# Banks returned earlier, one pool of places, memory keys after the projection and memory tokens also given transposed: a two-layer decoder trunk on one core

## The chip, the cores and the metric

The kernel runs on one core of a Trainium2 chip, in float32 and in the fp32r form of it that TensorE takes at one column per cycle. The metric is the time of one execution on the device in microseconds. PE is TensorE, DVE is VectorE, ACT is ScalarE, POOL is GpSimd and SP is the queue that issues nearly all DMAs.

## What is computed

Two layers act on x, 256 tokens of 1024 features. Each layer does three things in turn, each with a pre-RMS-norm and added to x.

- The mixer. In layer 0 it is one input projection for two groups of eight heads (A: an indexer scores all keys and each query keeps the best 64; B: causal attention within one block of 256) and one output projection over both. In layer 1 it is 16 heads in four groups with three branches (compressed blocks, selected blocks, a window), mixed by gates.
- Cross-attention with four heads of 128 to 256 memory tokens. The memory has its own RMS norm with a gain per layer; keys are normed per head.
- A SwiGLU feed-forward of width 2816.

```python
for i in range(DEPTH):
    h = rms_norm(x, norm_mix[i])
    x = x + (dsa_moba_mixer if i % 2 == 0 else nsa_mixer)(h, ...)
    x = x + memory_cross_attention(rms_norm(x, norm_mem[i]), rms_norm(mem, norm_mem_src[i]), ...)
    x = x + swiglu(rms_norm(x, norm_ffn[i]), ffn_w_in[i], ffn_w_out[i])

def memory_cross_attention(h, m, w_q, w_kv, w_o, q_norm, k_norm):
    q = rms_norm((h @ w_q).reshape(B, S, 4, 128), q_norm)
    k, v = _split(m @ w_kv, (512, 512))
    k = rms_norm(k.reshape(B, M, 4, 128), k_norm)
    p = softmax(einsum('bshd,bmhd->bhsm', q, k) * 128 ** -0.5)
    return einsum('bhsm,bmhd->bshd', p, v).reshape(B, S, 512) @ w_o
```

## The kernel before

**Tiles and matmuls.** The 256 tokens are two halves, t = 0 and 1, of 128 partitions. Every product with weights is done in three fp32r matmuls: the activation is split into a high and a low part, so is the weight, and high x high, high x low and low x high are added in one bank (mm3). A weight block is a list of units, each of two blocks of 128 input rows by up to 512 columns. A unit comes by DMA into one of three buffers `raw`; `pusher` writes its high part on ACT or DVE and its low part on DVE into one of six pairs `whl`. `gemm` takes one of two PSUM banks `mm`, walks over the units of its block and hands the bank to an evacuation thread `ev`; `both` does it for the two halves. The order of the weight blocks is the list that plan_block fills.

**Who sets the order.** The kernel is a set of generators (threads) run when it is built. Each yields an operation with an estimate of its cost on one or two engines, or a condition that must hold. `Steps.run` takes, at each step, the operation that can start first by the estimates in `Est` (within a small margin the one of the lowest rank; the main program has rank 4, evacuations and attention 2), and issues it. That fixes each engine's instruction order. On the chip the engines then run their lists in order and wait for each other's semaphores. A buffer is given back (`free`) when its last reader is issued, and until then no thread that wants it goes on. `haste` gives the pusher rank 0 only for the unit that the main program stands at, and 5 for those ahead of it.

**Buffers.** Four families of 2 KB per partition have fixed counts: 23 `slab` for queries, keys, memory, attention outputs and feed-forward activations, four `t2`, three `sn`, four `pt`, two `gv`. `t4` has two of 4 KB. PSUM has two banks each for `mm`, `sp` (scores), `tp` (transposes) and `po` (attention outputs).

**Layer 0's mixer** runs the blocks s (the indexer and A's key and value), aq, bk, bq, bv through `gemm`. Their evacuations copy the bank, square it, take the root of the mean square per head (`inv_rms`; the power on POOL), rotate, split and transpose. In `inv_rms` the bank is read by the copy and the square, but `free` is called by the caller after `inv_rms` has issued the power. `index` and `top` work out A's mask; `attention` does A for t = 0 and 1, then B. When the four pairs of heads of one branch and half are done, `finish` takes two slabs and splits the result into them (oT). After bq the thread `mem_prep` starts: it loads the memory (two DMAs of 512 KB into t4), squares it, transposes it in eight groups of four per two layers, multiplies by the gain on the way out of PSUM (`evac_gain`, through a `gv`) and splits into eight slabs (mT), which are held until the memory's values are done.

**The main program** (line 1502 on) does, per layer: the mixer, `mem_k` (the memory's key block: 24 matmuls per half of 128 memory tokens), `project` (the output projection: per half of the mix width and per t, waiting for that oT, 12 matmuls for each of two column blocks), `mem_attn` (query block mq, value block mv, output block mo) and `ffn`. The norm for the queries starts when the projection has been added to x.

Of the kernel before, what the change touches and what calls it, by code (L numbers as in the profile page):

```python
# [15 lines left out]
P = 128  # L16
D = 1024
# [36 lines left out]
NSLAB = 23  # L54
TAPS = 8
PTS = 4


class Op:
# [17 lines left out]
    def issue(self):  # L77
        e, outs, ins, cost, f = self.best()[2]
        self.est.issue(e, outs, ins, cost)
        f()  # L80
        for op in self.then:
            op.issue()
# [58 lines left out]
class Est:  # L141


    def __init__(self, nc):
        self.clk = {"PE": 0.0, "V": 0.0, "S": 0.0, "G": 0.0, "D": 0.0, "port": 0.0}
        self.wr, self.rd, self.busy = {}, {}, {}
        self.thin = False
        self.now = 0.0
# [46 lines left out]

    def issue(self, e, outs, ins, cost):
        lock = self.locks(e, outs, ins)
        t = max(self.clk[e], self.after(e, outs, ins), self.clk["port"] if lock else 0.0)
        if e == "PE":
            w = int(t / 3.413)  # L200
            c = cost * (1 if self.busy.get(w - 1, 0.0) > 1.26 else 2)
            n = 1
            for d in outs[0].shape[1:]:
                n *= d
            self.busy[w] = self.busy.get(w, 0.0) + cost * ins[0].shape[0] / P * min(1.0, n / P)
# [14 lines left out]
    class Engine:  # L220
# [3 lines left out]
        def __getattr__(self, name):  # L224
            f = getattr(self.e, name)

            def call(*a, **k):
# [9 lines left out]
                def do():  # L237
                    return f(*a, **{q: v() if q in ("start", "stop") and callable(v) else v for q, v in k.items()})  # L238
                return Op(self.est, [(self.n, outs, ins, self.cost(name, a, k, outs, ins), do)])
            return call  # L240

        def cost(self, name, a, k, outs, ins):
# [3 lines left out]
            if self.n == "PE":  # L246
                if name == "transpose":
                    return max(0.03, n * (0.00042 if ins[0].dtype == F32R else 0.00084))
                if k.get("tile_position", (0, 0))[1]:
                    return 0.012  # L250
                if ins[0].dtype == F32R:
                    return n * 0.00043 + 0.009
# [16 lines left out]
class Slots:  # L269
# [10 lines left out]
    def ready(self):  # L280
        return bool(self.open)
# [17 lines left out]

@with_exitstack  # L300
def trunk(ctx: ExitStack, tc: tile.TileContext, I, out):
# [37 lines left out]
    spawn = ck.spawn  # L339
    MM, SP, TP, PV = Slots(est, pp, "mm", 2), Slots(est, pp, "sp", 2), Slots(est, pp, "tp", 2), Slots(est, pp, "po", 2)  # L340
# [3 lines left out]
    GV = Slots(est, tp, "gv", 2)  # L344
# [127 lines left out]
    PO.memset(one, 1.0).issue()  # L472
    mhalf = cp.tile([P, 16], F32, name="mhalf")
# [18 lines left out]
    def tables():  # L492
# [20 lines left out]
        yield S.activation(cos, ang, AF.Sin)  # L513
        yield has(("mix0", 0), 2)
# [62 lines left out]
    def gemm(key, t, h, K, ev, need=None, part=None):  # L577
# [4 lines left out]
        for k0 in range(0, K, 2):  # L582
            u = yield from unit(plan_at[key] + k0 // 2)
            if need and k0 % 4 == 0:
# [7 lines left out]
        spawn(ev(ps[:, :n], free, t))  # L592

# [47 lines left out]

    def root(key, t):
# [126 lines left out]
    def mixer0():  # L769
# [100 lines left out]
        def ev_q(j, key):  # L870
            def ev(ps, free, t):
                q, qf = yield from T2.get([P, 8, HD])
                yield move(q.rearrange("p h d -> p (h d)"), ps)
                yield from inv_rms(ps, 8, HD, (yield from root("mix0", t))[0], 1.0, HD, rq[j, t])
                free()
# [13 lines left out]
        def ev_k(ps, free, t):  # L889
# [3 lines left out]
            yield from inv_rms(ps, 8, HD, (yield from root("mix0", t))[0], 1.0 / HD, 1.0, rk)  # L893
            free()
# [75 lines left out]
        spawn(mem_prep(0), 2)  # L970
# [22 lines left out]
    def mixer1():  # L993
# [92 lines left out]
        def ev_sw(br):  # L1086
            def ev(ps, free, t):
# [4 lines left out]
                yield from inv_rms(ps[:, :256], G, HD, v, 1.0 / HD, 1.0, rk[:, :G])  # L1092
                if br == 0:
                    yield S.activation(vv[:, t, :G, :], ps[:, 256:].rearrange("p (h d) -> p h d", h=G), AF.Copy, scale=r)
                free()
# [28 lines left out]
        def ev_q(j):  # L1124
            def ev(ps, free, t):
                q, qf = yield from T2.get([P, 8, HD])
                yield move(q.rearrange("p h d -> p (h d)"), ps)
                yield from inv_rms(ps, 8, HD, (yield from root("mix1", t))[0], 1.0, HD, rq[j, t])
                free()
# [128 lines left out]
        spawn(mem_prep(1), 2)  # L1258
# [4 lines left out]
    def mem_prep(L):  # L1263
        m = I["mem"][0].rearrange("(t p) d -> t p d", p=P)
        for t in range(NT):
            raw, rf = yield from T4.get([P, D])
            nc.sync.dma_start(raw, m[t])
            est.note(raw, est.wr, clk["PE"] + 6.0, "D")
            ss = tiny(2, "mss")
            for h in range(2):  # L1270
                rs = raw[:, 512 * h:512 * h + 512]
                junk, f = yield from T2.get([P, 512])
# [287 lines left out]
```

## Time and profile before

| | |
|---|---|
| time, median of 3 runs | 803.68 us (800.99 to 805.22) |
| profiled execution, its own time | 802.33 us |
| its span | 800.6 us |
| PE busy | 765.6 us, 96% of the span |
| DVE busy | 533.0 us, 67% |
| ACT busy | 436.7 us, 55% |
| POOL busy | 132.8 us, 17% |
| DMA | 121.27 MB, mean 151 GB/s |

The span runs from the first instruction to the last; the execution's own time is a little longer. A busy share is a mean over stages: layer 0's mixer lies in about 17 to 148 us, its memory attention to 194, its feed-forward to 385; layer 1's mixer to 562, its memory attention to 608 and its feed-forward to the end. PE's rows overlap, since matmuls are pipelined, so the time that a matmul costs is best read from one start to the next. Nearly all operations are issued by one line of the kernel, 238, so the rows are told apart by the tiles: mm is a projection bank, tp a transpose bank, sp scores, po attention outputs, whl a split weight, h the normed activations, slab, t and gv the buffers above.

### The profile page before, as it was taken

The page shows a single profiled execution, that of the slowest core. Times are in us where ns is not written, and L with a number is a line of the kernel's source. Part 1 is how long each engine was busy: PE and PEld are TensorE (multiplying, and loading weights), DVE is VectorE, ACT ScalarE, POOL GpSimd, SP SyncE. Part 2 cuts the span into 40 slices and gives each one's busy share as a digit, 9 for nine tenths or more (in the row PEclk, how much of TensorE's full clock was granted, in tenths as well). Part 3 has the DMA queues.
Part 4 walks back from the last instruction along what each step waited for, and adds up shares of the span by engine and source line. Part 5 has one row for each costly group of instructions (what it writes and reads, how often), then busy time and mean ns, then how long its engine had stood idle before and what let it go on. Part 6 is the DMA issues. An engine that isn't in the chain of part 4 may idle for free.

```text
span 800.6 us, 11834 instructions
## 1 busy us (share of the span) xinstructions
PE 765.6 (96%) x4259; PEld 635.5 (79%) x4259; DVE 533.0 (67%) x1088; ACT 436.7 (55%) x822; POOL 132.8 (17%) x194
## 2 busy tenths in 40 slices
PE   6988999999999999999998988999999999999998
PEld 5766788897888889788877767887897888889886
DVE  6888998868555554554726888886857565546541
ACT  5766985675543443443615677884656344435430
POOL 1665340100000000000016373340200000000000
PEclk9998999999999999999999998999999999999999
DMA  7633643426556645876414623033624665546751
GB/s 221 192 98 92 194 136 100 142 102 193 166 171 206 186 156 157 228 247 186 131 46 123 212 78 106 2 105 108 188 102 132 211 187 183 160 140 212 218 189 52
DMA packets 69482, 121.27 MB, mean 151 GB/s; under 512 B 8420, under 2 KB 15664, under 8 KB 69424
## 3 DMA queue, kind: packets, MB, share of 16 engines
q1 hardware_dynamic: 69392, 120.53, 48.8%
q8 instruction: 33, 0.54, 0.3%
q14 instruction: 25, 0.20, 0.1%
q0 software_dynamic: 32, 0.00, 0.0%
HBM read 119.46 MB, written 1.05 MB: 151 GB/s over the span
## 4 chain that ended last, share of the span: by engine, by line
PE 78%; DVE 8%; ACT 5%; DMA 5%; issue 2%; POOL 1%; SPq 0%; ACTq 0%; DVEq 0%; POOLq 0%
PE mm L238 58%; PE po L238 11%; PE tp L238 7%; PE sp L238 2%; DVE whl L238 2%; DVE slab L238 1%; ACT whl L238 1%; DMA raw<-in_ffn_w_in 1%; DMA raw<-in_ab_w_in 1%; ACT sn L238 1%; DMA raw<-in_nsa_w_in 1%; ACT slab L238 1%; DVE sn L238 1%; DVE kvT L238 1%; DVE hss L238 1%
## 5 line engine op out<-in xcount | busy, mean ns | idle before, releaser
L238 PE MATMUL mm<-whl,h 128*128 128x512 f32 (+3 forms) x1776 | 399.1, 379 | 10.1 <-DVE whl L238 9.1
L238 PEld LDWEIGHTS mm<-whl,h 128*128 128x128 f32 x1776 | 311.8, 189 | 69.9 <-DVE whl L238 10.9
L238 DVE TENSOR_TENSOR whl<-raw,whl 128x1024 fp32r<-128x1024 f32 (+3 forms) x232 | 271.3, 1174 | 143.3 <-ACT whl L238 139.0
L238 ACT ACTIVATE whl<-raw 128x1024 fp32r<-128x1024 f32 (+2 forms) x212 | 214.7, 1016 | 167.4 <-DMA raw<-in_ffn_w_in 42.0
L238 PE MATMUL mm<-whl,slab 128*128 128x512 f32 (+1 forms) x840 | 198.6, 375 | 2.0 <-ACT mvm L238 1.0
L238 PEld LDWEIGHTS mm<-whl,slab 128*128 128x128 f32 x840 | 141.7, 188 | 28.3 <-DVE x L238 1.8
L238 PE MATMUL po<-whl,slab 128*128 128x512 f32 x264 | 68.2, 396 | 0.0
L238 POOL TENSOR_TENSOR rh<-vh,mhalf 128x1 f32<-128x1 f32 x12 | 10.1, 845 | 326.7 <-DVE vh L238 310.5
L238 ACT ACTIVATE slab<-tp 128x256 fp32r<-128x256 f32 (+2 forms) x72 | 31.3, 463 | 50.9 <-PE tp L238 50.8
L238 PEld LDWEIGHTS po<-whl,slab 128*128 128x128 f32 x264 | 49.3, 188 | 11.4
L238 ACT ACTIVATE sn<-sn,mx 128x128 f32<-128x128 f32 (+1 forms) x96 | 42.7, 448 | 6.2 <-DVE mx L238 5.8
L238 POOL TENSOR_TENSOR sn<-sn,rc 128x512 f32<-128x512 f32 (+2 forms) x32 | 32.6, 1022 | 48.9 <-DVE rc L238 30.8
L238 PE MATMUL tp<-ident,t 128*128 128x128 f32 x224 | 35.5, 282 | 4.4 <-DVE slab L238 2.9
L238 PEld LDWEIGHTS tp<-ident,t 128*128 128x128 f32 x224 | 27.3, 143 | 11.8 <-POOL t L238 3.2
L238 DVE CUSTOM_DVE_ANT_0 sn<-sp,cm,rq 128x128 f32<-128x128 f32 (+1 forms) x80 | 30.6, 409 | 7.8 <-PE sp L238 6.6
L238 PE MATMUL tp<-ident,sn 128*128 128x128 f32 (+1 forms) x180 | 31.6, 288 | 2.1 <-POOL sn L238 1.4
L238 ACT ACTIVATE pt<-tp 128x512 f32<-128x512 f32 (+2 forms) x51 | 26.8, 535 | 11.7 <-PE tp L238 11.1
L238 DVE TENSOR_TENSOR x<-mm,x 128x512 f32<-128x512 f32 x36 | 24.5, 686 | 13.0 <-PE mm L238 12.9
L238 ACT ACTIVATE h<-gv 128x512 fp32r<-128x512 f32 x22 | 13.8, 628 | 30.9 <-DVE gv L238 30.9
L238 ACT ACTIVATE t<-mm,rh 128x512 f32<-128x512 f32 (+1 forms) x26 | 17.0, 654 | 24.7 <-PE mm L238 24.7
L238 ACT ACTIVATE t<-mm 128x512 f32<-128x512 f32 (+2 forms) x44 | 23.1, 557 | 9.1 <-PE mm L238 6.9
L238 PEld LDWEIGHTS tp<-ident,sn 128*128 128x128 f32 (+1 forms) x180 | 21.8, 146 | 7.5 <-POOL sn L238 2.3
(198 smaller groups left out, 667.9 us busy)
## 6 DMA issues: line engine op xcount, KB each, us to landing
raw<-in_ffn_w_in SPq DMA_DIRECT2D x80, 512.0 KB, 3.9
raw<-in_ffn_w_out SPq DMA_DIRECT2D x44, 512.0 KB, 4.4
raw<-in_ab_w_in SPq DMA_DIRECT2D x16, 512.0 KB, 3.7
raw<-in_mem_w_kv SPq DMA_DIRECT2D x16, 512.0 KB, 3.8
raw<-in_nsa_w_in SPq DMA_DIRECT2D x16, 512.0 KB, 4.1
raw<-in_ab_w_out SPq DMA_DIRECT2D x8, 512.0 KB, 3.7
raw<-in_mem_w_q SPq DMA_DIRECT2D x8, 512.0 KB, 3.8
raw<-in_mem_w_o SPq DMA_DIRECT2D x8, 512.0 KB, 4.1
```

Of the source, the lines that this page charges most:

```text
L238: return f(*a, **{q: v() if q in ("start", "stop") and callable(v) else v for q, v in k.items()})
```

## The change

- **Banks.** `inv_rms` takes `free` and calls it after the square. In layer 1's ev_sw the values are copied out ahead of it.
- **One pool.** slab, t2, sn, pt and gv are now kinds of one pool of 36 places. Each kind has a least number (23, 4, 3, 2, 1) that the others leave to it; the other three places go to whoever asks. The memory's values are two such places per layer where they were a tile.
- **Memory.** The host hands in the memory transposed as well (mem_t). `mem_prep` (now rank 3) loads a quarter of it per DMA, 256 KB, and writes the high and low parts straight from it (`gained`). The square sums come from the untransposed memory once, in layer 0 (`mem_root`), in four DMAs of 256 KB.
- **Order.** In each layer `mem_k` and its weight block come after `project`. Its gemm waits for mT two blocks of 128 at a time, and its evacuation for the root of the memory's norm.
- **Tables and estimates.** A one-element activation loads the Sin table at the start and the Exp table after the cosine. `Est` counts 1.28 for a table load, 0.235 for a matmul on a quarter of the array, and full cost in its model of PE's clock.

```diff
+PLACES = 36
+LEAST = {"slab": 23, "t2": 4, "sn": 3, "pt": 2, "gv": 1}
...
-            self.busy[w] = self.busy.get(w, 0.0) + cost * ins[0].shape[0] / P * min(1.0, n / P)
+            self.busy[w] = self.busy.get(w, 0.0) + cost
...
+class Kind:
+    def ready(self):
+        p = self.p
+        if p.used[self.k] < p.least[self.k]:
+            return True
+        return len(p.slots.open) > sum(max(0, p.least[k] - p.used[k]) for k in p.least)
...
+    def ready(func):
+        yield S.activation(warm, one, func)
...
-    SL = Slots(est, hp, "slab", NSLAB)
-    T2, T4, SN, PT = Slots(est, tp, "t2", 4), Slots(est, tp, "t4", 2), Slots(est, tp, "sn", 3), Slots(est, tp, "pt", PTS)
+    places = Places(est, hp, "place", PLACES, LEAST)
+    SL, T2, SN, PT, GV = (places.kind(k) for k in LEAST)
+    T4 = Slots(est, tp, "t4", 2)
...
-        plan_block((L, "mk"), I["mem_w_kv"][L], 0, 512, KD)
         for half in (0, 1):
             for c in (0, 1):
                 plan_block((L, "out", half, c), ...)
+        plan_block((L, "mk"), I["mem_w_kv"][L], 0, 512, KD)
...
+    S.activation(warm, one, AF.Sin).issue()
...
         yield S.activation(cos, ang, AF.Sin)
+        yield from ready(AF.Exp)
...
+    def gained(src, gain, hi, lo):
+        yield move(hi, src, gain)
+        yield V.scalar_tensor_tensor(lo, src, gain, hi.bitcast(F32), op0=OP.mult, op1=OP.subtract)
...
-    def inv_rms(ps, H, dh, v, mul, add_k, r):
+    def inv_rms(ps, H, dh, v, mul, add_k, r, free):
         sq, f = yield from T2.get([P, H, dh])
         yield S.activation(sq.rearrange("p h d -> p (h d)"), ps, AF.Square)
+        free()
...
     def mem_prep(L):
...
+        if L == 0:
+            spawn(mem_root())
+        for b in range(NB):
+            raw, rf = yield from T2.get([P, 2, SEQ])
+            nc.sync.dma_start(raw, I["mem_t"][:, 2 * b:2 * b + 2])
+            hi = yield from SL.get([P, 2, SEQ], F32R)
+            lo = yield from SL.get([P, 2, SEQ], F32R)
+            mT[b] = (hi, lo)
+            for j in range(2):
+                c = 32 + 8 * L + 2 * b + j
+                yield from gained(raw[:, j], gT[:, c:c + 1], hi[0][:, j], lo[0][:, j])
+            rf()
+            done(("mT", L))
...
-            yield from mem_k(L)
             ver += 2
             for t in range(NT):
                 spawn(norm(("mem", L), t, 16 + 8 * L, ver))
             yield from project(L)
+            yield from mem_k(L)
...
+    a["mem_t"] = np.ascontiguousarray(np.asarray(inputs["mem"])[0].reshape(SEQ, KD, P).transpose(2, 1, 0))
```

## Rows read from the trace of the kernel before

**Rows 1.** The page: engine, busy us (share of the span) and instructions.

```profile
PE 765.6 (96%) x4259; PEld 635.5 (79%) x4259; DVE 533.0 (67%) x1088; ACT 436.7 (55%) x822; POOL 132.8 (17%) x194
```

**Rows 2.** Stretches: length, busy us (instructions) of PE, PEld, DVE, ACT, POOL; clock, DMA.

```profile
66.90:84.10 17.20, 12.23 (x61) 9.09 (x59) 15.72 (x47) 12.25 (x24) 9.61 (x16) 0.80 0.26 81
...
94.50:134.50 40.00, 40.00 (x282) 32.65 (x281) 37.49 (x113) 32.35 (x83) 14.97 (x13) 1.00 0.38 110
134.50:148.20 13.70, 13.70 (x67) 11.20 (x66) 10.91 (x15) 7.22 (x11) 0.00 (x0) 1.00 0.53 162
...
420.00:445.00 25.00, 19.89 (x133) 17.66 (x132) 18.43 (x45) 14.12 (x32) 12.73 (x23) 1.00 0.44 125
...
467.00:498.70 31.70, 25.22 (x215) 21.67 (x215) 25.99 (x96) 24.34 (x74) 14.22 (x19) 0.84 0.24 84
498.70:545.00 46.30, 46.24 (x387) 38.96 (x385) 37.75 (x142) 35.35 (x107) 16.93 (x20) 1.00 0.15 47
```

**Rows 3.** PE's waits: engine and line waited for, us, times, longest.

```profile
PE mm L238 <- DVE whl L238: 9.1, 10, 1.5
...
PE mm L238 <- ACT vv L238: 1.0, 1, 1.0
```

**Rows 4.** PE timeline, layer 0: start, us, operation, count, [idle before, releaser].

```profile
70.21 0.91 PE L238 MATMUL tp<-ident,t 128*128 128x128 f32 x4 [2.24 <-DVE slab L238]
70.77 1.63 PE L238 MATMUL mm<-whl,h 128*128 128x512 f32 x3
...
95.42 0.60 PE L238 MATMUL tp<-ident,t 128*128 128x128 f32 x4
95.78 2.35 PE L238 MATMUL mm<-whl,slab 128*128 128x512 f32 x9
97.96 0.38 PE L238 MATMUL tp<-ident,sn 128*128 128x128 f32 x2
...
100.15 0.66 PE L238 MATMUL po<-pt,av 128*64 128x128 f32 x8
```

**Rows 5.** Groups on DVE, 75 to 108: busy us, mean ns, idle before.

```profile
L238 DVE TENSOR_TENSOR gv<-tp,gT 128x512 f32<-128x512 f32 x4 | 2.8, 688 | 0.6 <-PE tp L238 0.6
L238 DVE TENSOR_TENSOR slab<-gv,slab 128x512 fp32r<-128x512 f32 x4 | 2.7, 682 | 0.0
...
L238 DVE TENSOR_TENSOR vm<-mss 128x1 f32<-128x1 f32 x2 | 0.9, 428 | 0.0
...
L238 DVE SCALAR_TENSOR_TENSOR slab<-tp,kv,slab 128x256 fp32r<-128x256 f32 x2 | 0.9, 480 | 0.0
```

**Rows 6.** DMA issues of the memory: count, KB each, us to landing.

```profile
t<-in_mem SPq DMA_DIRECT2D x4, 512.0 KB, 6.5
```

**Rows 7.** ACT's timeline, the square of block bq's first half.

```profile
65.49 0.59 ACT L238 ACTIVATE t<-mm 128x512 f32<-128x512 f32 x1
```

**Rows 8.** POOL's timeline, the root of block bq's first half.

```profile
70.38 1.65 POOL L238 TENSOR_TENSOR rq<-hss,mhalf 128x8 f32<-128x8 f32 x1 [0.22 <-DVE hss L238]
```

**Rows 9.** DVE's timeline, two neighbouring low parts of weights.

```profile
61.37 1.21 DVE L238 TENSOR_TENSOR whl<-raw,whl 128x1024 fp32r<-128x1024 f32 x1
...
76.48 1.22 DVE L238 TENSOR_TENSOR whl<-raw,whl 128x1024 fp32r<-128x1024 f32 x1
```

**Rows 10.** Groups on PE, 94.5 to 108.3.

```profile
L238 PE MATMUL mm<-whl,slab 128*128 128x512 f32 x36 | 9.9, 408 | 0.0
```

**Rows 11.** ACT's timeline, the split of the first attention output.

```profile
106.76 0.59 ACT L238 ACTIVATE slab<-po 128x512 fp32r<-128x512 f32 x1
```

**Rows 12.** ACT's timeline, the Exp table and the first exponential.

```profile
83.64 1.28 ACT L238 ACT_TABLE_LOAD   x1
84.94 0.40 ACT L238 ACTIVATE sn<-sn,mx 128x128 f32<-128x128 f32 x1
```

**Rows 13.** PE's timeline, layer 1: a memory transpose, the first of the keys.

```profile
490.30 0.66 PE L238 MATMUL tp<-ident,t 128*128 128x128 f32 x4
...
498.69 0.72 PE L238 MATMUL mm<-whl,slab 128*128 128x512 f32 x2
```

More of the change, by code (lines that the diff above doesn't have):

```diff
@@ L16 @@
 P = 128
+NB = 4
 D = 1024
@@ L147, in __init__ @@
         self.thin = False
+        self.table = None
         self.now = 0.0
@@ L194, in locks, with load @@
         return e == "G"
+    def load(self, func):
+        table = {AF.Sin: "sin", AF.Exp: "exp", AF.Silu: "silu"}.get(func)
+        if table not in (None, self.table):
+            self.table = table
+            self.clk["S"] += 1.28
     def issue(self, e, outs, ins, cost):
@@ L250, in cost @@
                     return 0.012
+                if ins[0].shape[0] == 64 and outs[0].shape[0] == 64:
+                    return 0.235
                 if ins[0].dtype == F32R:
@@ L297, in get, with __init__, kind, take @@
         return self.take(shape, dt)
+class Places:
+    def __init__(self, est, pool, name, n, least):
+        self.slots, self.least, self.used = Slots(est, pool, name, n), least, dict.fromkeys(least, 0)
+    def kind(self, k):
+        return Kind(self, k)
+class Kind:
+    def __init__(self, places, k):
+        self.p, self.k = places, k
+    def ready(self):
[3 more added lines that the diff above has]
+        return len(p.slots.open) > sum(max(0, p.least[k] - p.used[k]) for k in p.least)
+    def take(self, shape, dt=F32):
+        self.p.used[self.k] += 1
+        t, f = self.p.slots.take(shape, dt)
+        def free():
+            f()
+            self.p.used[self.k] -= 1
+        return t, free
+    def get(self, shape, dt=F32):
+        yield self.ready
+        return self.take(shape, dt)
 @with_exitstack
@@ L592, in gemm, with pairs @@
         spawn(ev(ps[:, :n], free, t))
+    def pairs(key):
+        return lambda k0: has(key, 1 + k0 // 2)
     def both(key, h, K, ev):
@@ L1287, in msel @@
     def msel(t):
-        return lambda k: tuple(mT[t, k // 4][e][0][:, k % 4, :] for e in range(2))
+        return lambda k: tuple(mT[k // 2][e][0][:, k % 2, t * P:(t + 1) * P] for e in range(2))
     def mem_k(L):
@@ L1311, in mem_k @@
         for t in range(NT):
-            yield has(("mT", L, t))
-            yield from gemm((L, "mk"), t, msel(t), KD, ev)
+            yield from gemm((L, "mk"), t, msel(t), KD, ev, pairs(("mT", L)))
     def mem_attn(L):
-        vm = hp.tile([P, NT, MH, MD], F32, name="mvm")
+        vm = {}
         qT, rq = {}, [hp.tile([P, MH], F32, name=f"mrq{t}") for t in range(NT)]
@@ L1365, in mem_pv @@
             for i in range(2):
-                yield together([T.matmul(po[:, i, :], vm[:, b, h0 + i, :], pt[:, 2 * i + b, :], start=(b == 0), stop=(b == 1))
+                yield together([T.matmul(po[:, i, :], vm[b][0][:, h0 + i, :], pt[:, 2 * i + b, :], start=(b == 0), stop=(b == 1))
                                 for b in range(2)])
             ptf()
+            done(("mpv", L))
+            if has(("mpv", L), 2 * NT)():
+                for b in range(NT):
+                    vm[b][1]()
             hl, hf = yield from SL.get([P, 2, 2, P], F32R)
@@ L1375, in ev @@
             def ev(ps, free, t):
-                yield move(vm[:, t, 2 * p:2 * p + 2].rearrange("p h d -> p (h d)"), ps, mvr[t][1])
+                if p == 0:
+                    vm[t] = yield from SL.get([P, MH, MD])
+                yield lambda: t in vm
+                yield move(vm[t][0][:, 2 * p:2 * p + 2].rearrange("p h d -> p (h d)"), ps, mvr[t][1])
                 free()
@@ L1385, in mem_attn @@
                 yield from gemm((L, "mv"), t, msel(t), KD, ev_v(p), part=(256 * p, 256))
-        for t in range(NT):
-            for h in range(2):
-                for e in range(2):
-                    mT[t, h][e][1]()
+        for b in range(NB):
+            for e in range(2):
+                mT[b][e][1]()
         for p in range(2):
```

64 lines of the change are left out of this document (25 added, 39 removed).

## The prediction

> **What bounds the kernel now.** I read the page from the top, then the kernel stage by stage, then who ended TensorE's idle time, then single instructions around the parts of the change.
>
> The page says TensorE: 765.6 us busy of 800.6, 96% [rows 1], so the search is for the few stretches in which it isn't full; the stretches give the size [rows 2]. In layer 0's mixer, 66.9 to 84.1, PE is busy 12.2 of 17.2 us; from 94.5 to 148.2 it is full for 53.7 us. Layer 1's mixer has 5.1 us of idle time in 420 to 445 and 6.5 us in 467 to 498.7, and is full from 498.7 to 545. The feed-forward stages are full and the change doesn't touch them. The granted clock is 0.80 in 66.9 to 84.1 and 0.84 in 467 to 498.7: its levels are 2.4 and 1.2 GHz, so 40% of 17.2 us and 32% of 31.7 us went by at the lower one. The largest named cause of idle time is weight splits on VectorE, 9.1 us [rows 3]. So there are some 35 us of idle time to win, and only PE work removed, or a hole closed, shortens the time; a hole opened lengthens it at full price.
>
> **Memory transposed on the host.** It removes 32 PE transposes, 8 groups of four. A group holds PE for 0.35 us where PE is full (95.42 to 95.78, [rows 4]): 8 x 0.35 = 2.8 us. Two groups lie in the 66.9 to 84.1 hole and two around 490, where layer 1 also has idle time; these count in part. I take -2, bounds -1.4 and -2.8. It also takes eight multiplications by the gain off VectorE, and layer 1's squares off ScalarE. In layer 0, 75 to 108, VectorE spends 2.8 (gain) + 2.7 (low parts) + 0.9 us on the memory [rows 5]. The new form makes eight low parts of 256 columns per layer; the nearest row is 480 ns [rows 5], 3.8 us, beside eight high parts which either engine can take. It is moved to a lower rank, so most of it can fall after the attention. The loads on SP's queue go from four of 512 KB (6.5 us to landing, [rows 6]) to twelve of 256 KB; a load whose place is still being read holds the weight loads behind it. Three units of weights are always loaded ahead, so I cost it at nothing; without that cover each costs at most the longest weight wait, 1.5 us [rows 3], and I keep +3 for the range.
>
> **Early return of banks.** Block bq's first half in layer 0 shows it. Its square leaves ScalarE at 65.49 [rows 7], but the planner gives the bank back only with the root on GpSimd at 70.38 [rows 8], and the next block's first matmuls come at 70.77, after PE had stood 2.24 us [rows 4]. As the main program asks for no new weights meanwhile, VectorE makes no split between 61.37 and 76.48 [rows 9], and the matmuls after these wait for that too. With the bank back 4.9 us earlier this hole should shrink by some 3 us (bounds 0 and 5, the idle time of that stretch). But VectorE is 15.7 of 17.2 us busy there [rows 2], and what follows decides whether it counts (next part). In layer 1 the one wait for a bank that names its reader is 1.0 us (ACT vv, [rows 3]); the rest of 420 to 445 is the supply of weight halves. -1, bounds 0 and -3.
>
> **Memory's keys behind the projection.** This is the part that can hurt. From 94.5 the keys' 48 matmuls (24 for each half of the tokens) are what PE does while attention A waits for the other engines: up to 108.3, when the first attention output is split, 36 of them ran [rows 10]. Nine such matmuls take 2.18 us (95.78 to 97.96, [rows 4]), 0.242 each, so 36 x 0.242 = 8.7 us. After the change the main program stands at the projection until that output is there. Call this moment t1. What PE still has to do then is 53.7 us less the attention's own part before 108.3 (13.8 - 8.7 = 5.1) less one group of transposes (0.35) = 48.2 us, and the memory queries start at t1 + 48.2. They started at 148.2. So the move pays if t1 is under 100.0, and each microsecond beyond costs one.
>
> t1 is 108.3 now, but the products were done at 100.8 [rows 4]; the split starts on ScalarE at 106.76 [rows 11]. Between lies the slab count: at 100 four kinds of keys and queries hold 15 slabs and the memory 8, which is all 23, and the split needs two; they come when the second half's queries go, just ahead of the split. **The pool of places** ends this: of 36 places 33 are reserved by kind and three float, so the split can start at 100.8. With 1.5 us for it (106.76 to 108.3) t1 is 102.4. VectorE then loses 6.4 us of memory work ahead of it [rows 5], and from 94.5 to 134.5 it is 37.5 of 40 us busy [rows 2], and the Exp table, loaded at 83.64 right before the first exponential [rows 12], is now loaded early. All of that would give t1 = 94.7; none, 102.4. I take half, 98.5: the queries start at 146.7, -1.5 us; bounds -5.3 and, with t1 unmoved, +8.3. What the earlier banks win in front of 94.5 is not added: PE then only waits longer for t1.
>
> A rule to weigh here is in the Trainium skill, ScalarE: Activation LUTs, section What ACT_TABLE_LOAD costs: about 1.28 us for the load and 1.38 more to drain. The trace shows 1.28 and the exponential 0.02 us later [rows 12], no drain. By that page t1 would come 1.4 us earlier still and the sum would be 1.4 us lower, an estimate; I stay with the trace.
>
> In layer 1 the filler is no worse: before, the keys start at 498.69 because the memory is transposed late (490.30, [rows 13]); after, the projection's first quarter can start when the first output is split, about 491. By 545 both orders have 72 of the 144 matmuls (48 of the keys, 96 of the projection) at hand, so the stretch stays full. I take -1 for 467 to 498.7 (bounds 0 and -5), as the memory work leaves ScalarE and VectorE.
>
> **The rest.** The values of the memory move from a tile of their own to two places: nothing. PT falls from 4 sure places to 2 and GV from 2 to 1, each with the floating three: 0, at most +1 if they are taken. The square freed early adds no instruction. The new costs (matmuls on a quarter of the array, table loads, the clock) and ranks change only the planner's order; I take 0, and +-2 for the range.
>
> **Sum.** -2 (transposes) -1.5 (layer 0) -1 (420 to 445) -1 (467 to 498.7) = -5.5. The profiled execution took 802.33 us (800.6 of span and 1.7 around it): 796.8, and as it lies 1.35 below the median, 803.68, I say 797. Under 0.5% (4 us) can hardly be told from no change here.
>
> **Rivals.**
> *The lost filler (slower).* t1 stays near 108.3: half of the floating places go to other kinds, or the memory's eight slabs are taken before the split's two, and PE stands at the projection. Price 8.3 in layer 0, less 1 for the other transposes; with nothing gained in layer 1 and 1 of the 3 us of the queue, 802.3 + 8.3 - 1 + 1 = 810.6, say 811. It decides from t1 = 104 on (100.0 plus the 4 us won elsewhere). For it: the filler is 8.7 us of work in a full stretch. Against: the delay from 100.8 to 106.76 has the slab count as its cause, and that count is raised. 12%.
> The Trainium skill, TensorE: Matmul & The Clock Gate, section Part 1: The HAM clock gate, says that the low clock is the default and that activity lifts it; a PE with only attention to do could fall back to 1.2 GHz. The trace agrees in a like stretch: 0.80 where PE was busy 71% [rows 2]. By that rule the attention's 5.1 us of PE work would take up to twice that and this rival would end at up to 816.
>
> *Holes close and open again elsewhere (no change).* VectorE bounds layer 0's mixer (91% busy in 66.9 to 84.1, 94% in 94.5 to 134.5, [rows 2]); the hole at 67 only moves to t1 (t1 about 101), layer 1 keeps its holes, and of the transposes 2 us remain: 802.3 - 2 + 1 = 801. For: VectorE's busy share. Against: its work shrinks too. 28%.
>
> *All bounds on the good side.* t1 = 94.7 (-5.3), 467 to 498.7 with most of its 6.5 us of idle time gone (-5), -2 for the transposes and -2 in 420 to 445: 788. For: in that stretch the memory's gains and squares fall between attention steps. Against: its chain is the rotation on GpSimd and the softmax, which nothing here shortens. 12%.
>
> *The forecast*, 797, its own range 793 to 800: 48%.
>
> **How the numbers follow.** Faster by over 0.5% (under 799.7): the good case, and most of the forecast's 48%: 12 + 45 = 57%; slower (over 807.7): 12% of the lost filler, plus 1% for the order: 13%; the rest, 30%, within. The range reaches over the no-change case and into the lost filler, and down to the good one: 787 to 806.
>
> **What would show it.** No transposes of memory in the trace. The first projection matmuls at about 98 to 99, with PE idle ahead of them no more than 4 us; the memory keys after the last of the projection; the queries' start before 148. The next block's matmuls right behind bq's, without the 2.24 us wait, and no 15 us pause in the weight splits. The first Exp load near 25 us. I am wrong if PE's idle time in 90 to 125 grows beyond 6 us, if the total idle time stays at 35 us, or if layer 1's 467 to 498.7 gets longer.

## The result, and the profile after

The changed kernel takes 793.29 us (median of 4 runs, 792.18 to 794.83), the kernel before 802.77 beside it (4 runs, 800.99 to 805.22): a ratio of 0.9881, with a 95% interval of 0.9848 to 0.9914. That is 1.2% faster, by 9.5 us; 797 was forecast, with a range of 787 to 806. The size is near and the sign right, but that is luck in part: the sum hides two errors that cancel. Stage by stage (profiled execution against profiled execution, by the first matmul of each block in the timelines):

```
                                             before    after   change
start to the feed-forward of layer 0         194.01   200.02    +6.0
  (in it: to the memory queries of layer 0   148.25   153.68    +5.4)
layer 1, window keys to first queries         19.38    14.63    -4.8
layer 1, first queries to memory queries     122.55   111.97   -10.6
everything else                                                  0.0
span                                          800.6    791.3    -9.3
```

Layer 0 lost 6 us, where 1.5 were to be won, and layer 1 won some 15, where 2 were expected beside the transposes.

The page's first part (engine, busy us, share of the span, instructions) answers to [rows 1]:

```profile
PE 759.2 (96%) x4227; PEld 630.1 (80%) x4227; DVE 529.8 (67%) x1088; ACT 427.2 (54%) x813; POOL 141.2 (18%) x198
```

Exactly the 32 transposes have gone (4259 to 4227), VectorE's work is 3.2 us less, and the idle time of PE is 791.3 - 759.2 = 32.1 us where it was 35.0. So 6.4 us of the 9.3 are busy time of PE and 2.9 idle time, but the engines' totals do not show where they went. The stretches do. The kernel before, between those first matmuls (columns as in [rows 2]):

```profile
70.77:148.25 77.48, 74.75 (x458) 60.17 (x457) 71.53 (x203) 59.21 (x140) 23.45 (x28) 0.96 0.42 127
419.79:439.17 19.38, 15.61 (x116) 14.48 (x114) 13.06 (x34) 9.82 (x23) 12.82 (x23) 1.00 0.45 132
439.17:561.72 122.55, 114.58 (x810) 95.59 (x809) 100.11 (x309) 87.64 (x234) 45.18 (x54) 0.96 0.31 100
```

The same three stretches after (block bv's first matmul to the queries of layer 0; window keys to first queries; first queries to memory queries of layer 1), and with them the windows that answer to [rows 2]:

```profile
66.35:153.68 87.33, 76.96 (x448) 61.24 (x446) 78.44 (x230) 58.21 (x141) 29.09 (x33) 0.94 0.40 126
84.00:100.00 16.00, 9.59 (x57) 7.02 (x55) 15.70 (x64) 11.92 (x37) 6.29 (x8) 0.83 0.31 98
90.00:125.00 35.00, 30.19 (x208) 24.15 (x207) 31.05 (x106) 24.87 (x75) 13.21 (x14) 0.85 0.33 106
100.00:115.00 15.00, 13.82 (x100) 11.70 (x100) 12.98 (x48) 10.32 (x34) 6.50 (x8) 0.84 0.32 97
425.35:439.98 14.63, 14.18 (x107) 13.49 (x106) 9.65 (x24) 9.97 (x22) 13.27 (x23) 1.00 0.53 150
439.98:551.95 111.97, 108.89 (x798) 90.90 (x797) 96.08 (x308) 85.99 (x235) 44.14 (x55) 1.00 0.37 114
467.00:498.70 31.70, 29.88 (x292) 25.94 (x290) 29.69 (x141) 30.67 (x109) 21.10 (x25) 1.00 0.19 60
498.70:545.00 46.30, 46.29 (x343) 38.54 (x342) 38.54 (x103) 31.38 (x80) 9.59 (x12) 1.00 0.33 100
```

Read them as length = PE busy + PE idle. In layer 0, idle time went from 2.7 (77.48 - 74.75) to 10.4 us, and busy time rose by 2.2 although four groups of transposes had left it: the granted clock is 0.94 in place of 0.96, so a larger part of the stretch went by at the lower of its two levels. In layer 1's attention the two move the other way: idle 8.0 to 3.1, busy 114.6 to 108.9, of which the four groups of transposes are 4 x 0.35 = 1.4 us [rows 4]. The other 4.3 go with the clock, 0.96 to 1.00. Of layer 0's idle time 6.4 us lie in 84 to 100, where VectorE is full (15.70 of 16) and PE does only attention. PE's waits in 84 to 115 (who waits, for whom, us, times, longest):

```profile
PE sp L246 <- DVE mx L246: 3.4, 3, 2.0
PE tp L246 <- POOL place L246: 1.4, 2, 1.0
PE po L246 <- ACT place L246: 1.3, 2, 0.8
PE mm L246 <- ACT place L246: 1.2, 1, 1.2
```

and the end of that hole on PE's timeline, up to the projection's first matmuls, with the split that they wait for on ACT's:

```profile
91.17 1.53 PE L246 MATMUL tp<-ident,place 128*128 128x128 f32 x4
92.35 2.06 PE L246 MATMUL sp<-place,place 128*128 128x256 f32 x8
94.34 0.77 PE L246 MATMUL po<-place,av 128*64 128x128 f32 x8
97.16 2.01 PE L246 MATMUL sp<-place,place 128*128 128x256 f32 x8 [2.05 <-DVE mx L246]
100.36 1.22 PE L246 MATMUL mm<-whl,place 128*128 128x512 f32 x2 [1.20 <-ACT place L246]
```

```profile
99.73 0.58 ACT L246 ACTIVATE place<-po 128x512 fp32r<-128x512 f32 x1
```

From 84 to 100.36 there is no `mm` on PE: the main program stands at the projection, and the keys are behind it. In the kernel before, block bv ran up to 94.5, as it had started 4.4 us later, and the keys did PE's work from there [rows 10].

### The profile page after: what moved, and what is told of

It reads as the page before. It is cut to its first block, busy times and chain, and to the rows that moved or that the text cites. A ratio compares the mean times of both kernels' runs of the same rounds, so it can differ in the third digit from the quotient of the medians.

```text
span 791.3 us, 11761 instructions
## 1 busy us (share of the span) xinstructions
PE 759.2 (96%) x4227; PEld 630.1 (80%) x4227; DVE 529.8 (67%) x1088; ACT 427.2 (54%) x813; POOL 141.2 (18%) x198
## 4 chain that ended last, share of the span: by engine, by line
PE 73%; DVE 9%; DMA 6%; ACT 6%; issue 3%; POOL 1%; SPq 1%; ACTq 0%; POOLq 0%; DVEq 0%
PE mm L246 56%; PE po L246 9%; PE tp L246 6%; DVE whl L246 4%; ACT place L246 3%; DMA raw<-in_ffn_w_out 3%; PE sp L246 3%; ACT whl L246 2%; DVE place L246 2%; DMA raw<-in_ab_w_in 1%; DVE kvT L246 1%; DMA raw<-in_nsa_w_in 1%; DMA raw<-in_mem_w_kv 1%; DVE m L246 0%; DMA raw<-in_ffn_w_in 0%
## 5 line engine op out<-in xcount | busy, mean ns | idle before, releaser
L246 ACT ACTIVATE whl<-raw 128x1024 fp32r<-128x1024 f32 (+3 forms) x208 | 210.4, 1014 | 164.6 <-PE mm L246 39.8
L246 PE MATMUL mm<-whl,place 128*128 128x512 f32 (+1 forms) x840 | 194.5, 375 | 2.0 <-ACT place L246 1.2
L246 PEld LDWEIGHTS mm<-whl,place 128*128 128x128 f32 x840 | 142.6, 189 | 29.2 <-DVE x L246 1.6
L246 ACT ACTIVATE place<-tp 128x512 f32<-128x512 f32 (+4 forms) x123 | 57.3, 492 | 66.6 <-PE tp L246 66.4
L246 PE MATMUL po<-whl,place 128*128 128x512 f32 x264 | 68.1, 396 | 0.0
L246 PEld LDWEIGHTS po<-whl,place 128*128 128x128 f32 x264 | 49.3, 188 | 11.3
L246 PE MATMUL tp<-ident,place 128*128 128x128 f32 (+1 forms) x340 | 54.3, 280 | 4.1 <-DVE place L246 1.8
L246 PEld LDWEIGHTS tp<-ident,place 128*128 128x128 f32 (+1 forms) x340 | 40.1, 143 | 14.2 <-POOL place L246 2.9
L246 ACT ACTIVATE place<-place,mx 128x128 f32<-128x128 f32 (+1 forms) x96 | 42.7, 450 | 6.4 <-DVE mx L246 4.7
L246 POOL TENSOR_TENSOR place<-place,rc 128x512 f32<-128x512 f32 (+2 forms) x36 | 32.4, 908 | 34.6 <-DVE rc L246 20.1
```

## The experiments

All are timed beside the kernel before. A column of the table names a stretch: "queries 0" is the start of layer 0's memory queries, "kw to q0" and "q0 to queries 1" are the two stretches of layer 1 above, all from the one profiled execution of each (those of mem_pe and l0_est are 2.4 and 1.9 us above the medians of their runs, the others lie within 1.2).

```
                 time us  ratio   95% interval     queries 0  kw to q0  q0 to queries 1
before                                              148.3      19.4      122.6
changed          793.29   0.9881  0.9848 - 0.9914   153.7      14.6      112.0
keys_first_l0    794.01   0.9904  0.9882 - 0.9926   154.4      14.6      112.3
keys_first       800.59   0.9989  0.9977 - 1.0000   154.3      14.6      117.2
late_banks       794.46   0.9913  0.9893 - 0.9933   153.4      16.2      110.7
est_old          792.95   0.9894  0.9877 - 0.9911   150.2      16.1      114.5
b_l1             801.72   0.9993  0.9972 - 1.0013   148.3      20.9      119.7
b_mem_l1         801.66   0.9983  0.9965 - 1.0002   155.5      19.4      116.6
mem_pe           800.00   0.9968  0.9948 - 0.9989   156.2      14.6      115.3
fixed            794.04   0.9890  0.9860 - 0.9919   152.9      14.0      117.7
l0_early         791.26   0.9865  0.9836 - 0.9894   150.6      14.6      112.2
l0_early2        791.99   0.9880  0.9843 - 0.9916   151.5      14.6      112.1
l0_est           790.31   0.9846  0.9819 - 0.9872   151.0      14.6      111.7
l0_loads         785.31   0.9781  0.9756 - 0.9806   145.6      14.6      112.1
```

**The order, layer 0 alone and both layers** (the changed kernel with the keys and their weights ahead of the projection again):

```
-            yield from project(L)
+            if L == 0: yield from mem_k(L)      (keys_first: in both layers)
             yield from project(L)
-            yield from mem_k(L)
+            if L == 1: yield from mem_k(L)
```

> After the change, with layer 0's memory keys back ahead of the projection. Layer 0 reached its feed-forward 6.0 us later than before the change. Theory A (lost filler): the order is the cause, PE stands at the projection from 84 to 100; with the keys there the queries start 5 us earlier and the time falls by 4 to 6 us, to about 788. Rival B (VectorE bounds the stretch): the keys only fill time in which the attention is slowed by their own evacuations and splits; less than 1.5 us changes.

> After the change, with the keys ahead of the projection in both layers. Theory A: layer 0 as in the other run; layer 1 loses part of its 15.7 us, as its memory must be ready at about 476 and is made in the middle of the attention: 2 to 5 us above the run with layer 0 alone, about 791. Rival: in layer 1 too the keys are filler for PE between 476 and 496, and it is at or below the other run, 786 to 788.

Putting the keys ahead in layer 0 gave nothing back, as its rival had it: the queries start at 154.4. In its timeline the keys run from 83.4 to 129.7, since the memory's preparation, now at the low rank, isn't done (its last low part on VectorE is made at about 120); the main program stands at the keys instead of the projection. So the order alone is not the cause of layer 0's loss. In layer 1 the order is worth 6.6 us (794.0 against 800.6), somewhat more than the 2 to 5 expected.

**Banks returned late** (`free` again behind the power that `inv_rms` issues; the copy of the values, which was moved ahead of `inv_rms`, left there) and **the planner's costs as before**:

```
-        free()
         ss = tiny(H, "hss")
         ...
         yield from pow_half(r, ss)
+        free()
```

```
-            self.busy[w] = ... + cost
+            self.busy[w] = ... + cost * ins[0].shape[0] / P * min(1.0, n / P)
-                if ins[0].shape[0] == 64 and outs[0].shape[0] == 64: return 0.235
-        if e == "S": self.est.load(getattr(f, "func", None))
```

> After the change, but every bank is given back only after the root, as before. Theory A (banks): block bv ends near 92 instead of 84 and layer 1's blocks q0 and q1 lose their overlap with the attention; 4 to 8 us slower, about 799, most of it in layer 1. Rival C (the planner's new costs make layer 1's gain): within 1.5 us of 793.

> After the change, with the planner's costs as before: its clock model, its matmul cost on a quarter of the array, and no cost for table loads (the two early table loads stay). Rival C: layer 1's gain of 15.7 us goes by half or more, 8 us or more slower, about 801. Theory A: the costs only shuffle, within 2 us of 793.

Neither changes the time by an amount these intervals can tell from none, as the second theory of each had it. Block bv starts at 66.1 with late banks, as in the changed kernel (66.35; 70.77 before), so the hole ahead of it closes without the early return too. The old costs lose less in layer 0 (queries at 150.2, and 2.5 us lost up to the feed-forward in place of 6.0) and win less in layer 1. So the new costs have a share in layer 0's loss.

**One part put on the kernel before:** the new order in layer 1 (b_l1), then that and the transposed memory (b_mem_l1); and **one part taken out of the changed kernel:** the transposed memory (mem_pe), the pool (fixed).

```
b_l1:      plan_block((L, "mk"), ...) and mem_k(L) behind the projection where L == 1
b_mem_l1:  b_l1, and mem_root, mem_prep, msel, gained, pairs of the changed kernel;
           mem_prep(0) at rank 2, mem_prep(1) at rank 3
mem_pe:    mem_prep and msel of the kernel before, spawn(mem_prep(L), 2)
fixed:     SL = Slots(est, hp, "slab", 23); T2, SN, PT, GV = Slots(...) of 4, 3, 4, 2
           vm: a tile of its own for each half
```

> The kernel before with one part of the change alone: in layer 1 the memory's keys and their weights stand behind the projection; layer 0, the memory's transposes on TensorE, the banks and the places as before. Theory (the order alone): putting the keys ahead again in the changed kernel took 6.6 us of layer 1's gain away, so the order alone gives about that: 794 to 797, queries of layer 1 5 to 8 us earlier than before (561.7), the low clock between 469 and 487 gone. Rival (order and late memory together): the memory's transposes, gains and low parts at 470 to 500 still delay the attention, so the projection starts little earlier: 799 to 803.

> The kernel before with two parts of the change: the memory tokens transposed on the host (prepared at the middle rank in layer 0, at the low rank in layer 1) and, in layer 1 alone, the memory's keys behind the projection. Banks, places, planner's costs and layer 0's order as before. Theory (the two are one gain): the order alone gave nothing and the transposes alone are PE work of 2.8 us, but together they take all memory work out of layer 1's attention: the stretch from the first queries to the memory queries of layer 1, 122.6 us before and 112.0 after, comes to 112 to 115, total 791 to 795. Rival (every part needs the pool and banks): that stretch stays at 116 to 120, total 796 to 799.

> The changed kernel with the memory transposed by TensorE again (32 transposes, eight gains, layer 1's squares; preparation at the middle rank as before), all else as changed: the keys behind the projection in both layers, early banks, the pool. Theory (work only): TensorE's time grows by its transposes, 2 to 3 us, and no hole changes: 795 to 797. Rival (their place counts): the gains and low parts sit in layer 1 at 470 to 500 and in layer 0 at 75 to 108, ahead of attention on a full VectorE, and open holes too: 798 to 803, with layer 1's queries 3 us or more later than in the changed kernel.

> The changed kernel with the five families of places of the kernel before (23 slabs, 4 + 3 + 4 + 2 of the others, the memory's values in tiles of their own) in place of the one pool. Theory (the pool feeds VectorE): the 4.8 us won between the window's keys and the first queries of layer 1 (19.4 before, 14.6 after) and a part of the attention's gain come from floating places: kw to q0 back at 18 to 20 us, the first attention output of layer 0 split again near 106 (101.5 after), total 797 to 801. Rival (the pool is idle): places are seldom short once the memory comes late, kw to q0 stays under 16 us, total 792 to 795.

Stretch "q0 to queries 1" in four of these, each from its own trace (b_l1, b_mem_l1, mem_pe, fixed):

```profile
441.72:561.44 119.72, 112.97 (x807) 94.17 (x805) 99.56 (x306) 83.52 (x227) 45.05 (x53) 0.97 0.32 102
```

```profile
444.67:561.25 116.58, 110.23 (x794) 91.47 (x793) 102.11 (x312) 84.18 (x226) 38.90 (x46) 0.99 0.33 106
```

```profile
446.86:562.17 115.31, 110.79 (x814) 92.39 (x813) 100.20 (x315) 86.70 (x237) 45.01 (x55) 1.00 0.36 111
```

```profile
436.85:554.50 117.65, 111.34 (x802) 91.90 (x801) 103.65 (x320) 87.15 (x235) 39.30 (x50) 0.99 0.35 109
```

Here the gain adds up from three parts: 122.6 before, 119.7 with the order (-2.8), 116.6 with the transposed memory too (-3.1), 112.0 with the rest (-4.6). From the other side, taking out the order costs 5.2 here (117.2 in keys_first), the transposed memory 3.3, the pool 5.7. No part that was taken out is worth more than 5.7 of the 10.6, and the order put on alone gives 2.8. The expectation that order and memory were one gain missed this stretch by 2 to 5 us; its rival, 116 to 120, had the stretch right, and both had the total too low. Over the whole program, the intervals of b_l1 and b_mem_l1 contain no change at all, for b_l1 as its rival had it: 1.3 and 6.0 us won in layer 1's attention and its neighbours went in holes elsewhere, in b_mem_l1 in layer 0, whose queries come 7.2 us late. mem_pe ended where its rival said (798 to 803). Its 800.0 is not all the price of the transposes: in the profiled execution 4.5 us lie between layer 0's feed-forward and layer 1's first block (195.25 against 190.75 us), a stretch that no other run has over 193.7; why there stays open. fixed made up for 3.1 of its 5.7 us in small pieces (layer 0's feed-forward starts 1.4 us sooner, the stretch from there to layer 1 is 1.0 shorter, kw to q0 0.7), and by the medians the pool is worth 0.8 us, which the intervals can't tell from none; that is the rival's 792 to 795.

**Layer 0's memory ready in time.** l0_early puts layer 0's keys ahead again and prepares the memory at the middle rank; l0_early2 starts that two blocks earlier; l0_est adds the old costs until layer 1.

```
-        spawn(mem_prep(0), 3)
+        spawn(mem_prep(0), 2)        (l0_early2: ahead of block bk)
```

> The changed kernel, but in layer 0 the memory's keys stand ahead of the projection again and the memory's preparation runs at the middle rank (2) instead of the low one (3), so that the keys have their operand. Theory (starved PE): layer 0's loss is idle time of TensorE between block bv and the memory queries, 10.4 us against 2.7 in the kernel before, since at 84 to 115 us it has neither the projection's operand nor the keys'; with the keys ready they fill it: queries of layer 0 at 145 to 149 us (153.7 in the changed kernel), idle time of that stretch under 5 us, total 786 to 789. Rival (VectorE sets the pace): VectorE is full from 66 to 118 us in either order, so the memory's low parts, done ahead of the attention, delay the attention by as much as they feed TensorE: queries at 152 to 156, total 792 to 796. In both layer 1 is as in the changed kernel (a gain of about 15 us from layer 0's feed-forward to the memory queries of layer 1).

> As the run above, with the preparation of layer 0's memory started two blocks earlier (ahead of block bk, at about 36 us, where VectorE is 22.5 of 26 us busy instead of full). Starved PE: queries of layer 0 at 144 to 148, total 785 to 788. VectorE sets the pace: the work is only moved to a place ahead of the attention, block bv starts later by up to 4 us, queries at 151 to 156, total 791 to 796.

> The run with layer 0's keys ahead and its memory prepared early (791.3), with the planner's costs of the kernel before in use until layer 1 begins. With the old costs in both layers, layer 0 lost 2.5 us instead of 6.0, with the early memory 3.3; layer 1 lost 1 to 3 us by the old costs. Theory (the two gains in layer 0 are of different holes): queries of layer 0 at 146 to 149, total 787 to 790. Rival (VectorE sets the pace and the order only moves holes): queries at 150 to 153, total 790.5 to 794.

The first came out between its two theories: queries at 150.6 and idle time of 8.3 us from block bv to them. Started earlier, the preparation only moved the hole (block bv starts at 72.2, the queries at 151.5), as the theory that VectorE sets the pace had it. The old costs in layer 0 added nothing to it (l0_est: queries at 151.0, 790.31 us), so the two don't add up, as its rival had it. The trace of l0_early shows why the keys still wait. The loads of the transposed memory on SP (start, us, operation, count):

```profile
62.77 0.46 SPq L1346 DMA_DIRECT2D place<-in_mem_t  x1
...
75.77 0.46 SPq L1346 DMA_DIRECT2D place<-in_mem_t  x1
...
88.55 0.90 SPq L1346 DMA_DIRECT2D place<-in_mem_t  x2
```

and the last low part that comes of them on DVE:

```profile
103.67 0.48 DVE L246 SCALAR_TENSOR_TENSOR place<-place,gT,place 128x256 fp32r<-128x256 f32 x1
```

One thread loads a quarter, waits, uses it, and then asks for the next. A quarter holds two of the eight blocks of features for all 256 tokens, so even the first half's keys need all four, at 104. In the kernel before, memory came by token halves: the first was ready in the low part at 82.2 to 82.9 and the second at 98.8 to 99.5, by the same rows of DVE that [rows 5] group.

**Four loads at once** (on l0_early; layer 1 as changed):

```
+        def piece(b):
             hi, lo = two slabs; raw = a t2 place
             nc.sync.dma_start(raw, I["mem_t"][:, 2 * b:2 * b + 2])
             ... gained(...) twice
+            done(("mT", L, b))
+        for b in range(NB):
+            if L == 0: spawn(piece(b), 2)
+            else: yield from piece(b)
```

> The run with layer 0's keys ahead and its memory prepared early (791.3 us), where the four quarters of the transposed memory are loaded by four threads, each as soon as it gets its places, in place of one thread that loads a quarter, waits for it, uses it and then loads the next. There the last low part was made at 103.7 us, and as every quarter holds features of all tokens, even the first half's keys need it; in the kernel before the first half's operand was there at 81 and the second's at 98. Theory (the keys' operand comes too late to be a filler, by serial loads): last low part by 95, the keys done by 110 (118.4 there), idle time between block bv and the queries 8.3 down to under 6 us, queries at 145 to 148.5 (150.6 there), total 786 to 789.5. Rival (VectorE sets the pace): the low parts only move ahead of the attention's work on a full VectorE, queries at 149.5 to 153, total 790 to 794.

785.31 us, ratio 0.9781 (0.9756 to 0.9806): faster than the kernel before by 2.2%, and faster than the changed kernel, whose interval (0.9848 to 0.9914) it doesn't touch. Layer 1's two stretches are as in the changed kernel (14.6 and 112.1), so the gain lies in layer 0. The queries and the idle time are as the theory had them, the total is 0.7 us under its range. The four loads are issued at once, and the last low part is at 87.93:

```profile
63.58 1.85 SPq L1348 DMA_DIRECT2D place<-in_mem_t  x4
```

```profile
87.93 0.47 DVE L246 SCALAR_TENSOR_TENSOR place<-place,gT,place 128x256 fp32r<-128x256 f32 x1
```

The stretch from block bv to the queries, and 84 to 100 in it, first l0_early, then l0_loads:

```profile
65.94:150.59 84.65, 76.40 (x447) 59.80 (x446) 75.45 (x224) 59.47 (x145) 27.58 (x32) 0.94 0.39 129
84.00:100.00 16.00, 10.40 (x49) 7.21 (x49) 14.58 (x59) 11.33 (x32) 3.83 (x7) 0.71 0.35 117
```

```profile
66.25:145.57 79.32, 73.69 (x447) 57.24 (x446) 73.62 (x223) 59.84 (x146) 22.28 (x29) 1.00 0.44 140
84.00:100.00 16.00, 14.98 (x82) 10.92 (x80) 15.37 (x53) 14.02 (x37) 5.19 (x9) 1.00 0.64 200
```

With VectorE as full as in the others (15.37 of 16), PE is busy 14.98 us of 84 to 100 in place of 9.59 in the changed kernel and 10.40 in l0_early, and the clock stays at its higher level. 40 of the 48 key matmuls run there. Its timeline is keys between attention steps:

```profile
91.46 0.48 PE L246 MATMUL mm<-whl,place 128*128 128x512 f32 x1
92.00 0.44 PE L246 MATMUL tp<-ident,place 128*128 128x128 f32 x2
92.91 0.66 PE L246 MATMUL po<-place,av 128*64 128x128 f32 x8 [0.47 <-ACT place L246]
93.51 3.06 PE L246 MATMUL mm<-whl,place 128*128 128x512 f32 x12
```

So keys with their operand in time give back all that layer 0 lost, and more: 153.7 to 145.6 for the queries (busy 76.96 to 73.69, idle 10.4 to 5.6), with the kernel before at 148.3. The order alone (keys_first_l0) gave nothing, and the order with an operand that is complete only at 104 (l0_early) 3.1 us. The rival, that VectorE sets the pace whatever PE is given, had the queries at 149.5 at the least and misses by 4 us. That a lighter VectorE has a smaller share in it is not excluded: from block bv to the queries it works 73.62 us in place of 78.44, in part because five high parts of the memory (1.7 us) have gone from it to ScalarE. Nor was the early operand tried with the keys left behind the projection.

## Why the prediction was right, and which terms were not

**Memory transposed on the host, -2: right.** 32 matmuls have gone; by the prediction's 0.35 us a group, 1.4 us of layer 1's busy time are theirs, an estimate. The low parts cost 0.48 us each, as taken. The loads hold no weights back: PE's waits for split weights fell from 9.1 us [rows 3] to 6.9. What was not seen is the new layout's own price: quarters of features, loaded one after the other, make all keys wait for the last quarter. "Most of it can fall after the attention" was true of the low rank, and in a kernel with a hole at 84 to 100 that is no merit.

**Early banks, -1: the stretch is right in kind, the cause only in part.** From the window's keys to the first queries of layer 1, 4.8 us were won, and PE's idle time there fell from 3.8 to 0.5 us. Returning the banks late again costs 1.6 us in that stretch; over the whole program the difference is 1.2 us by the medians and 2.6 by the ratios, with intervals that overlap. The old costs cost 1.4 us in that stretch too. The one wait for a bank that names its reader, on ACT's copy of the values [rows 3], is gone in the changed kernel and in all its variants, late banks included; in them that copy stands ahead of the root. The two kernels built on the kernel before without the new position of the copy, b_l1 and b_mem_l1, still have it. The copy's position was not tried by itself. The hole at 67 shrank as said (idle 5.0 us in 66.9 to 84.1 before, 2.8 from block bv to 84 after), and block bv starts as early with late banks, old costs, fixed places or TensorE's transposes; which part does it stays open (the early Exp table was in all of these).

**Keys behind the projection, layer 0: the failed step.** t1, when the first output is split, was forecast at 98.5; the split starts at 99.73 and the projection's first matmul is at 100.36, so t1 was near. The step that failed is "the queries start at t1 + 48.2": from 100.36 it took 53.3 us. The windows from t1 to the queries, before and after (columns as in [rows 2]):

```profile
108.30:148.25 39.95, 39.95 (x264) 32.46 (x265) 34.71 (x91) 27.57 (x68) 7.62 (x7) 1.00 0.39 113
```

```profile
100.36:153.68 53.32, 52.50 (x317) 42.69 (x317) 45.01 (x114) 34.48 (x82) 12.56 (x14) 0.96 0.40 122
```

The 48.2 is the 39.95 of the first line with 36 key matmuls added, 8.7 us, and one group of transposes taken off. It supposed that at t1 the attention would be as far as it was at 108.3 before, and PE as full behind it. The second line has 53 matmuls more, not 36: some 17 more of the attention were still to come. PE ran them at a granted clock of 0.84 (100 to 115) and waited for 0.8 us in all. So of the 5.1 us that the step lacked, 0.8 are idle time and 4.3 busy time. By estimate the clock is about half of the 4.3: 0.84 over 15 us means 32% of them, 4.8 us, at half the rate, which is 2.4 us; the attention's matmuls are the rest. The idle time in front of t1, 9.6 of the 10.4 us, is not what failed: that block bv's early start (4.4 us) would be lost waiting for t1 was forecast. Of the signs that the prediction named, two failed with this step: the queries did not start before 148, and PE was idle for 6.4 us, not at most 4, in 84 to 100.

Nor did t1 come near 98.5 by the cause that the prediction gave. It put the step from 106.76 to 100.8 down to the pool. Without the pool (fixed) the split still starts at 101.92 and the projection at 102.66; with the pool but the memory prepared by TensorE at the middle rank (mem_pe) they start at 104.24 and 110.41:

```profile
101.92 0.68 DVE L246 CAST slab<-po 128x512 fp32r<-128x512 f32 x1
102.66 0.73 PE L246 MATMUL mm<-whl,slab 128*128 128x512 f32 x2
```

```profile
104.24 0.57 ACT L246 ACTIVATE place<-po 128x512 fp32r<-128x512 f32 x1
110.41 0.48 PE L246 MATMUL mm<-whl,place 128*128 128x512 f32 x1
```

So, taken out one at a time, the pool is worth 2.3 us of the projection's start, and the memory's late and lighter preparation up to 10. Two rivals had parts of what happened in layer 0. The lost filler named the mechanism and priced it at 8.3 us from t1 alone; it came with t1 near 100, at 5.4 us for the queries, and the total ended on the other side because layer 1 paid for it. The no-change case said that the hole at 67 would only move to t1, near 101. The bound set for idle time in 90 to 125, 6 us, was not passed (35.00 less 30.19 busy, 4.8): it did not cover the idle time before 90 nor the lower clock.

**Layer 1, 467 to 498.7, -1: the right place, mis-sized by its clock.** Idle time fell from 6.5 to 1.8 us, within the bound of 5, and the clock rose from 0.84 to 1.00. The prediction read the 0.84 and priced only idle time; 32% of 31.7 us at the lower of two levels is 10 us in which work took longer. From first queries to memory queries that made -10.6, in near equal parts idle time and busy time. The stretch up to 545 stayed full, as said (46.29 of 46.30), but that both orders would have 72 of the 144 matmuls at hand by 545 held for the kernel before alone (78 ran); after, 115 of projection and keys had run by then, since more of the attention was done by 498.7 (292 matmuls in 467 to 498.7 in place of 215).

**The rest, 0: right for the total.** Old costs and fixed places end within 1 us of the changed kernel. The Exp table loads at 25.32.

In 84 to 100 the granted clock is 1.00 where PE is busy for 14.98 us (l0_loads), 0.83 with 9.59 (changed) and 0.71 with 10.40 (l0_early), while VectorE is busy for 15.37, 15.70 and 14.58. By the Trainium skill, TensorE: Matmul & The Clock Gate, section Part 1: The HAM clock gate, the low clock is the default and activity lifts it. The traces agree: the nearly full stretch has the high level throughout, the two with holes don't, though busy time alone doesn't order these two.

## What to carry to other kernels

Matmuls that can run without the critical chain are worth keeping at hand where another engine sets the pace, so before moving or delaying them, ask per stage what PE has to do there. Here the same order won 6.6 us in layer 1; in layer 0, together with a later memory, it went with a loss of 6, and turning the order back gave nothing until the operand came in time too. A filler also has to have its operand in time: issue its loads at once rather than one after the other, and let a piece hold what one product needs. Where the granted clock is below 1 in a stretch, price the busy time beside the idle time: in layer 1's attention closing the holes gave back both.

## What was not expected of the hardware

The same root on GpSimd, 128 x 8, took 1.65 us before [rows 8] and 2.55 us after, where VectorE multiplies 128 x 1024 beside it from 63.59 on:

```profile
63.76 2.55 POOL L246 TENSOR_TENSOR rq<-hss,mhalf 128x8 f32<-128x8 f32 x1 [0.33 <-DVE hss L246]
```

```profile
63.59 1.22 DVE L246 TENSOR_TENSOR t<-place,rk 128x1024 f32<-128x1024 f32 x1
```

One pair is no proof that they disturb each other, and it wasn't tried by itself, but the kept traces hold 140 such roots. All 41 that start while a TENSOR_TENSOR of 128 x 1024 is already running on VectorE take 2.54 to 2.88 us; none of the 56 with no such instruction beside them takes over 1.82, and of the 43 beside which VectorE's starts later 41 stay under 2. So the longer time goes with VectorE having started first. And SP issues in order: in the changed kernel the third quarter of the memory was issued only behind five weight loads, which took 14.84 us of the queue, and 0.09 us after the last of them:

```profile
93.11 14.84 SPq L438 DMA_DIRECT2D raw<-in_ab_w_out  x5
108.04 0.42 SPq L1343 DMA_DIRECT2D place<-in_mem_t  x1
```
